# Loading the first 1 MB of a batch-norm kernel by four transfers of every fourth partition in place of one

## The chip, the cores and the metric

The kernel runs on one core of a Trainium2 chip. The metric is the device time in microseconds (us) of one launch. A profile of one execution shows a span (first to last instruction) that is some 1.8 us shorter than that time.

## The reference

```python
batch, channels, h, w = 32, 128, 32, 32      # x: 16.78 MB of float32
normalized = (x - running_mean) / np.sqrt(running_var + eps)
scaled = normalized * gamma + beta           # all per channel
return np.maximum(scaled, 0)
```

So 16.78 MB are read and 16.78 MB written, with a multiply-add and a maximum for each element in between.

## The kernel before

A row is one (batch, channel) image of 1,024 floats, 4 KB. Partition p holds 16 consecutive rows, 64 KB that are contiguous in HBM, and there are T = 2 such blocks. `PIECES` cuts the 16 rows of a block into pieces, the first ones small so that ScalarE can begin early. All loads are issued by SyncE, all stores and the four small parameter loads by ScalarE. Everything fits in SBUF at once, so no load waits for a buffer.

```python
PIECES = (((0, 2), (2, 4), (4, 8), (8, 16)), ((0, 8), (8, 16)))
STORE_CUTS = {(0, 1)}
...
for t in range(T):
    for a, b in PIECES[t]:
        xt = data.tile([P, b - a, HW], F32, name=f"x{t}_{a}")
        nc.sync.dma_start(out=xt, in_=xr[t, :, a:b, :])
        tiles.append((t, a, b, xt))
raw = params.tile([Q, 4, J], F32, name="raw")
for k, src in enumerate((running_var, gamma, running_mean, beta)):
    nc.scalar.dma_start(out=raw[:, k, :], in_=src.rearrange("(q j) -> q j", j=J))
...                                          # scale and bias of every channel
for t, a, b, xt in tiles:
    first = a
    for j in range(a, b):
        nc.scalar.activation(out=xt[:, j - a, :], in_=xt[:, j - a, :], func=ACTF.Relu,
                             bias=bias_t[:, j : j + 1], scale=scale_t[:, j : j + 1])
        if j + 1 == b or (t, j + 1) in STORE_CUTS:
            nc.scalar.dma_start(out=outr[t, :, first : j + 1, :], in_=xt[:, first - a : j + 1 - a, :])
            first = j + 1
```

The kernel names no semaphore. The framework hands out eight for the transfers of these two queues and reuses them; a transfer that gets a used one waits until the earlier transfer has landed.

## Time and profile before

| | before |
|---|---|
| time, median | 83.73 us (83.72 to 83.98, 3 runs) |
| span | 81.9 us |
| ScalarE busy | 38.5 us |
| share of the 16 DMA engines, loads + stores | 48.4% + 47.8% |
| first packet of x begins | 1.84 us |
| last completions of the 16 engines | 80.28 to 80.60 us |

The prediction shows the views. One more line is needed to compare with: how long SyncE's queue is busy with one issue. It comes from the view of the load's source line; the three durations are shortest, median and longest in ns, then the first and last start in us.

```profile
L52 SPq DMA_DIRECT2D x<-in_x_dram x6: 328/398/678, 0.8 to 8.0; - x6
```

The first three of these six, by the trace's records, began at 0.807, 1.229 and 1.706 us and took 372, 428 and 424 ns.

### The profile page before, as it was taken

What the parts mean: (1) busy time and instruction counts of PE and PEld (TensorE: products, weight loads), DVE (VectorE), ACT (ScalarE), POOL (GpSimd) and SP (SyncE); (2) the same over time, 40 slices, a digit from 0 to 9 for tenths busy, and PEclk for the clock granted to TensorE, in tenths of its full rate; (3) what the DMA queues carried; (4) which work ended last, traced back from release to release, by engine and by line L of the source; (5) the groups of instructions that cost most, each with busy time, mean ns of one, the idle gap of its engine ahead of it and who ended that gap; (6) DMA issues with size and microseconds to landing.
All of it is one profiled execution on the core that took longest, in us unless ns stands there. A gap on an engine that the chain in (4) does not pass through costs nothing.

```text
span 81.9 us, 119 instructions
## 1 busy us (share of the span) xinstructions
PE 0.7 (1%) x2; PEld 0.5 (1%) x2; DVE 0.8 (1%) x5; ACT 38.5 (47%) x34; POOL 0.8 (1%) x6
## 2 busy tenths in 40 slices
PE   0002000000000000000000000000000000000000
PEld 0002000000000000000000000000000000000000
DVE  0000300000000000000000000000000000000000
ACT  0600377799039999199994199993000000000000
POOL 3000000000000000000000000000000000000000
DMA  2899999989899999979789798996999899799690
GB/s 32 328 425 472 408 448 448 512 352 494 370 448 416 446 418 396 500 296 600 320 380 580 304 464 384 512 512 288 480 512 400 368 512 448 320 512 496 272 512 0
DMA packets 1936, 33.56 MB, mean 410 GB/s; under 512 B 272, under 2 KB 272, under 8 KB 528
## 3 DMA queue, kind: packets, MB, share of 16 engines
q1 hardware_dynamic: 864, 16.78, 48.4%
q10 hardware_dynamic: 1072, 16.78, 47.8%
HBM read 16.78 MB, written 16.78 MB: 410 GB/s over the span
## 4 chain that ended last, share of the span: by engine, by line
DMA 56%; ACT 11%; SPq 0%; issue 0%
DMA x<-in_x_dram 56%; ACT x L96 11%; SPq L52 0%
## 5 line engine op out<-in xcount | busy, mean ns | idle before, releaser
L96 ACT ACTIVATE x<-x,bias_t,scale_t 128x1024 f32<-128x1024 f32 x32 | 37.0, 1228 | 10.3 <-DMA x<-in_x_dram 7.9
L82 ACT ACT_TABLE_LOAD x1 | 1.3, 1283 | 2.6 <-issue 2.6
L82 ACT ACTIVATE std_t<-cols,eps_t 128x16 f32<-128x16 f32 x1 | 0.3, 273 | 4.5 <-PE cols L74 4.5
L74 PE MATMUL cols<-raw,rep 8*128 8x64 f32 x2 | 0.7, 428 | 7.7 <-DMA raw<-in_beta_dram 7.7
L74 PEld LDWEIGHTS cols<-raw,rep 8*128 8x128 f32 x2 | 0.5, 304 | 7.7 <-issue 7.7
L64 POOL TENSOR_SCALAR_AFFINE_SELECT rep<-rep 8x128 f32<-8x128 f32 x1 | 0.4, 392 | 0.1
L84 DVE RECIPROCAL rstd_t<-std_t 128x16 f32<-128x16 f32 x1 | 0.3, 254 | 7.8 <-ACT std_t L82 7.8
L63 POOL MEMSET rep<- 8x128 f32 x1 | 0.2, 195 | 0.3 <-POOLq L124 0.3
L86 DVE TENSOR_TENSOR scale_t<-cols,rstd_t 128x16 f32<-128x16 f32 x1 | 0.2, 175 | 0.1
L90 DVE TENSOR_TENSOR bias_t<-cols,ms_t 128x16 f32<-128x16 f32 x1 | 0.2, 175 | 0.0
L88 DVE TENSOR_TENSOR ms_t<-cols,scale_t 128x16 f32<-128x16 f32 x1 | 0.2, 175 | 0.0
L124 POOL MEMSET const-bfloat16-1.0<- 128x1 bf16 x1 | 0.1, 106 | 0.0
L124 POOL MEMSET const-uint8-127<- 128x1 uint8 x1 | 0.1, 106 | 0.0
L124 POOL MEMSET const-float32-0.0<- 128x1 f32 x1 | 0.1, 103 | 0.3 <-issue 0.3
L124 POOL MEMSET const-float32-1.0<- 128x1 f32 x1 | 0.1, 103 | 0.0
L61 DVE MEMSET eps_t<- 128x1 f32 x1 | 0.1, 59 | 0.9 <-PEq L124 0.9
## 6 DMA issues: line engine op xcount, KB each, us to landing
x<-in_x_dram SPq DMA_DIRECT2D x3, 4096.0 KB, 38.8
out_dram<-x ACTq DMA_DIRECT2D x3, 4096.0 KB, 27.9
x<-in_x_dram SPq DMA_DIRECT2D x2, 1024.0 KB, 5.7
x<-in_x_dram SPq DMA_DIRECT2D x1, 2048.0 KB, 11.2
out_dram<-x ACTq DMA_DIRECT2D x1, 2048.0 KB
out_dram<-x ACTq DMA_DIRECT2D x2, 512.0 KB, 18.8
out_dram<-x ACTq DMA_DIRECT2D x1, 1024.0 KB
raw<-in_running_var_dram ACTq DMA_DIRECT2D x1, 0.5 KB
```

The lines of the kernel that those rows point to most:

```text
L61: nc.vector.memset(eps_t, float(eps))
L63: nc.gpsimd.memset(rep, 1.0)
L64: nc.gpsimd.affine_select(out=rep, in_=rep, compare_op=mybir.AluOpType.is_equal, fill=0.0, base=0, pattern=[[0, P // Q], [-1, Q]], channel ...
L74: nc.tensor.matmul(cols.rearrange("p k j -> p (k j)"), rep.rearrange("q r s -> q (r s)"), raw.rearrange("q k j -> q (k j)"), start=True, s ...
L82: nc.scalar.activation(out=std_t, in_=cols[:, 0, :], func=ACTF.Sqrt, bias=eps_t[:, 0:1], scale=1.0)
L84: nc.vector.reciprocal(out=rstd_t, in_=std_t)
L86: nc.vector.tensor_mul(out=scale_t, in0=cols[:, 1, :], in1=rstd_t)
L88: nc.vector.tensor_mul(out=ms_t, in0=cols[:, 2, :], in1=scale_t)
L90: nc.vector.tensor_sub(out=bias_t, in0=cols[:, 3, :], in1=ms_t)
L96: nc.scalar.activation(out=xt[:, j - a, :], in_=xt[:, j - a, :], func=ACTF.Relu, bias=bias_t[:, j : j + 1], scale=scale_t[:, j : j + 1],)
L124: nc = _bacc.Bacc("TRN2", target_bir_lowering=False, num_devices=1)
```

## The change

The intent is to let all 16 DMA engines start sooner.

```diff
+SEED = 4
...
             xt = data.tile([P, b - a, HW], F32, name=f"x{t}_{a}")
-            nc.sync.dma_start(out=xt, in_=xr[t, :, a:b, :])
+            n = SEED if (t, a) == (0, 0) else 1
+            for s in range(n):
+                nc.sync.dma_start(out=xt[s::n], in_=xr[t, s::n, a:b, :])
```

## The prediction

> **What bounds the kernel now.** I read the view of cores first: 81.9 us from first to last instruction at clock 1.000, 1.83 us below the timed 83.73 us. I then read the page from the top, to see which engine could be the bound. No compute engine is: ScalarE is busy 38.5 us of 81.9, in 32 activations of 1.23 us, and everything else is under 1 us. The DMA rows of the page are different.
>
> ```profile
> DMA  2899999989899999979789798996999899799690
> ...
> DMA packets 1936, 33.56 MB, mean 410 GB/s; under 512 B 272, under 2 KB 272, under 8 KB 528
> ...
> q1 hardware_dynamic: 864, 16.78, 48.4%
> q10 hardware_dynamic: 1072, 16.78, 47.8%
> ```
>
> The first row is the mean share of the 16 DMA engines in 40 slices of 2.05 us: low in the first slice and zero in the last, and between them high, with dips that come from how a long packet is credited to slices. The two queues, loads (q1) and stores (q10), take 48.4 + 47.8 = 96.2% of the engines' span, 78.8 us. Only about 3.1 us of the whole program is not DMA time. Next I asked in which stretches it lies, by the busy time of the engines in chosen windows (columns: window, length, five engines' busy us and counts, clock, DMA share, GB/s; a packet's bytes are credited to the window in which it begins).
>
> ```profile
> 1.60:1.80 0.20, 0.00 (x0) 0.00 (x0) 0.00 (x0) 0.00 (x0) 0.00 (x0) 1.00 0.03 2
> 1.80:2.00 0.20, 0.00 (x0) 0.00 (x0) 0.00 (x0) 0.00 (x0) 0.00 (x0) 1.00 1.97 287
> 2.00:2.20 0.20, 0.00 (x0) 0.00 (x0) 0.00 (x0) 0.00 (x0) 0.00 (x0) 1.00 0.99 164
> 2.20:2.40 0.20, 0.00 (x0) 0.00 (x0) 0.00 (x0) 0.00 (x0) 0.00 (x0) 1.00 0.31 82
> 2.40:2.60 0.20, 0.00 (x0) 0.00 (x0) 0.00 (x0) 0.00 (x0) 0.00 (x0) 1.00 0.30 123
> 2.60:2.80 0.20, 0.00 (x0) 0.00 (x0) 0.00 (x0) 0.18 (x1) 0.00 (x0) 1.00 0.82 328
> 2.80:3.00 0.20, 0.00 (x0) 0.00 (x0) 0.00 (x0) 0.20 (x1) 0.00 (x0) 1.00 1.01 410
> 3.00:4.80 1.80, 0.00 (x0) 0.00 (x0) 0.00 (x0) 0.90 (x1) 0.00 (x0) 1.00 0.98 414
> 4.80:42.00 37.20, 0.65 (x2) 0.49 (x2) 0.78 (x4) 26.10 (x24) 0.00 (x0) 1.00 1.03 438
> 42.00:78.00 36.00, 0.00 (x0) 0.00 (x0) 0.00 (x0) 11.13 (x10) 0.00 (x0) 1.00 1.00 431
> ```
>
> From 3.0 us to 78 us the engines run at 414 to 438 GB/s without a hole; it matters little whether they carry loads, stores or both. Nothing moves before 1.8 us. Between 1.8 and 2.8 us is a ramp. Those two places, and some 1.3 us after the last packet, are all there is to win, and the change works on the ramp.
>
> The trace's packet records show the ramp in detail. Each of the first load's 128 partitions is one packet of 8 KB. The 16 engines begin their first one at 1.844 to 2.509 us: one after another, over 0.665 us. These first packets take 0.31 to 1.03 us where each later one takes 0.309 us; the early starters are the slow ones, and all 16 end between 2.670 and 2.998 us. After that each engine runs packet on packet: the 16 first-load completions leave at 4.836 to 5.136 us, and the very last completions of the program at 80.279 to 80.604 us. The spread among engines, 0.30 us at the beginning, is 0.33 us at the end. So each engine has its own chain of fixed work, and the program ends when the one that started worst ends. Its effective start is 5.136 - 8 x 0.309 = 2.66 us, and from there to 80.604 us it works 77.94 us. By packets of 32 KB at 1.21 us, its 2.10 MB would take 64 x 1.21 = 77.4 us, so it hardly ever idles.
>
> The page's chain of waits tells the same only in part:
>
> ```profile
> 0.81 0.37 SPq L52
> 1.18 0.05 issue
> 1.23 6.74 DMA x<-in_x_dram
> 7.97 0.02 issue
> 7.99 38.77 DMA x<-in_x_dram
> 46.76 0.03 issue
> 46.79 9.16 ACT x L96 x8
> ```
>
> It goes through the last load (issued at 7.99 us because its semaphore was in use) and the last eight activations, then stops at the last store, whose transfer it doesn't follow. I don't take this chain as the bound. When the last activation ends at 55.95 us, the store queue still holds about 6.4 MB: by then some (55.97 - 2.5) x 0.43 = 23.0 MB have moved, 16.78 MB of them loads, so 6.2 MB of the 12.6 MB of stores issued earlier. Earlier or later activations therefore wouldn't change the end.
>
> **What the skill says.** "DMA: Bandwidth & Descriptors", section "The descriptor swizzle", gives for a 128-partition transfer the engine of a partition as 8 * (partition >> 6) + ((partition >> 2) & 7): groups of four neighbours go to one engine. Every fourth partition then gives each of the 16 engines exactly two rows, which must be the reason for the stride. The same page, section "Why a DMA increments its semaphore by 16 and not by 1", has the number of engines as the largest k up to 16 that divides the slowest dimension of both sides; 32 rows still give 16. The trace of before agrees for 128 rows (16 engines, eight packets each); nothing in it shows 32. "SBUF — State Buffer", section "The DMA setup-cost knee", advises one large transfer in place of several because each pays about 2 us. That is latency of a single transfer; here the transfers overlap in the queue, and at the border of two loads (4.836 us) the next packet begins 6 ns after the completion packet, so I don't charge it. "Perfetto Trace Analysis", section "DMA Optimizations", says that splitting may let some transfers start sooner[...].
>
> **The change, part by part.** Removed: one 1 MB load. Added: four of 256 KB, so three more issues on SyncE's queue and 3 x 16 = 48 completion packets. Bytes, data packets (128 of 8 KB), activations and stores stay.
>
> *Gain.* The start-up stagger of 0.665 us belongs to 128 rows. If it goes with the rows, 32 rows take 0.665 / 4 = 0.17 us, and the last engine begins at 1.844 + 0.17 = 2.01 us in place of 2.509. In before the first packets end 0.16 to 0.49 us after the last engine has begun; the same here gives 2.17 to 2.50 us, so the worst engine gains 2.998 - 2.50 = 0.50 us. The most that is possible is a start of every engine at 1.844 us without slow packets: 2.66 - 1.84 = 0.82 us, 1.0% of the time. If the slow first packets come from something else (the generator still has the other 96 rows to do in the same 0.7 us, or the memory is slow at first whatever is asked), the gain is nearly 0. I take the middle, 0.28 us.
>
> *Cost on the engines.* Three more completions per engine, 9 ns each: 0.03 us, all on the path.
>
> *Issue.* SyncE's queue issued its first four loads at 0.81, 1.23, 1.71 and 2.21 us; issue to first packet was 1.844 - 0.807 = 1.04 us. So the four small loads bring packets from about 1.85, 2.27, 2.75 and 3.2 us, and the second piece, issued at about 2.65 us in place of 1.23, from 3.7 us. One small load is two packets per engine, 0.62 us, more than the 0.42 to 0.50 us between issues. An engine that ends its first packet at 2.5 us has work to 2.8, 3.4, 4.0 and 4.65 us: each next load is there 0.5 us or more before it is needed. No cost.
>
> *Compute.* The parameter loads, which end at 7.6 us and hold TensorE (7.7 us of wait), sat behind the first load's packets and may land earlier. Activations and stores then start earlier than 9.72 us. By the store backlog above this is worth nothing at the end.
>
> Sum: -0.28 + 0.03 = -0.25 us; 83.73 gives 83.48.
>
> **Rivals.** (1) *Nothing but reordering*: descriptor generation for 128 rows takes as long as before and the packets crawl until it is through; time 83.7 to 83.8. For it: the early starters' packets took up to 1.03 us while those that began at 2.41 us took 0.307 to 0.342. Against: engines that already have a full packet's descriptor should be able to run it. (2) *A wait for a semaphore starves the queue.* The kernel already shows such waits:
>
> ```profile
> SPq L52 <- DMA raw<-in_running_mean_dram: 4.1, 1, 4.1
> ...
> SPq L52 <- DMA x<-in_x_dram: 0.7, 1, 0.7
> ```
>
> Loads reuse semaphores of earlier transfers, and three more transfers bring reuse forward. If the second piece waits for the first small load (about 3.1 us), it's still in time at 4.1; if for the last one (about 5.0 us), the engines would stand still for some 1.4 us: 84.9. In before the first reuse waited for a parameter load that had landed at 2.19 us, so I expect the harmless kind. (3) *The 32 rows don't spread as I assume*, for instance so that two engines write to the same group of partitions at once or only eight engines work. 1 MB at half rate is 2.45 us more: 86.1. The stride looks chosen against this. (4) *The whole ramp is gained*: 82.9.
>
> **Range and chances.** Between rival 1 and the full stagger gain lie 83.2 to 83.8; a little more for (4) and for a mild form of (2) gives 82.95 to 83.95 as the range for 8 in 10. Faster by over 2% would need 1.67 us, twice the largest possible gain: 0.01. Slower by over 2% needs rival 3, or 2 at its worst: 0.04. The rest, 0.95, is within 2%.
>
> **What would show it.** Right: in the windows of the changed kernel, the rate from 2.0 to 2.8 us is up; the first completions of the last small load leave near 4.5 us in place of 4.836 to 5.136; the last packets end as much earlier; 1,984 DMA packets (48 more); queue shares as before; no hole between 3 and 5 us. Wrong: engines' first packets still ending near 2.7 to 3.0 us (rival 1), a hole near 4 to 6 us with a wait on SyncE's queue (rival 2), or packets of 8 KB at 0.6 us, or on fewer engines (rival 3).

## The result and the profile after

| | before | after |
|---|---|---|
| median of 6 runs | 83.77 us (83.72 to 84.06) | 87.45 us (86.88 to 87.70) |
| span | 81.9 us | 85.6 us |
| ratio | | 1.0426 (1.039 to 1.0462) |

A ratio here is the mean time of one kernel's runs over that of the other's runs of the same rounds, so not quite the ratio of the medians. Executions over 1.5% slower than the fastest of the same kernel are left out of the means. The predicted time was 83.48 us, with a range to 83.95: the change costs 3.7 us where a small gain was expected.

The page of the changed kernel, in the lines that answer to those of before:

```profile
DMA  0799999999999999999999899998999999999910
...
DMA packets 1984, 33.56 MB, mean 392 GB/s; under 512 B 320, under 2 KB 320, under 8 KB 576
...
q1 hardware_dynamic: 912, 16.78, 47.2%
q10 hardware_dynamic: 1072, 16.78, 45.7%
```

The 48 more packets are the completions of three more transfers. The row of shares now begins with an empty slice (2.14 us each). The row hardly shows the rest of the loss: it ends in 9, 1 and 0, although one engine works until 84.12 us, 1.5 us longer than the second last. The windows at the start say more (columns as in the prediction).

```profile
1.80:2.00 0.20, 0.00 (x0) 0.00 (x0) 0.00 (x0) 0.00 (x0) 0.00 (x0) 1.00 0.01 0
2.00:2.20 0.20, 0.00 (x0) 0.00 (x0) 0.00 (x0) 0.00 (x0) 0.00 (x0) 1.00 0.95 205
...
2.60:2.80 0.20, 0.00 (x0) 0.00 (x0) 0.00 (x0) 0.09 (x1) 0.00 (x0) 1.00 0.68 287
2.80:3.00 0.20, 0.00 (x0) 0.00 (x0) 0.00 (x0) 0.20 (x1) 0.00 (x0) 1.00 0.40 165
3.00:4.80 1.80, 0.00 (x0) 0.00 (x0) 0.00 (x0) 0.99 (x1) 0.00 (x0) 1.00 0.84 265
4.80:6.60 1.80, 0.65 (x2) 0.49 (x2) 0.00 (x0) 0.27 (x1) 0.00 (x0) 1.00 0.93 341
6.60:8.40 1.80, 0.00 (x0) 0.00 (x0) 0.78 (x4) 0.00 (x0) 0.00 (x0) 1.00 0.99 405
8.40:42.00 33.60, 0.00 (x0) 0.00 (x0) 0.00 (x0) 21.25 (x19) 0.00 (x0) 1.00 1.02 432
```

No packet of a load begins before 2.0 us, where before had 287 GB/s from 1.8 us on. From 3.0 to 4.8 us the rate is 265 GB/s against 414 in before, and it doesn't reach 430 until after 8 us. The share of busy engines (0.84, then 0.93) falls less than the rate: engines stand still, and besides that packets take longer. After the first packets the fifth microsecond is the worst. Here it is in before, then in the changed kernel:

```profile
4.00:5.00 1.00, 0.00 (x0) 0.00 (x0) 0.00 (x0) 0.00 (x0) 0.00 (x0) 1.00 1.01 418
```

```profile
4.00:5.00 1.00, 0.00 (x0) 0.00 (x0) 0.00 (x0) 0.00 (x0) 0.00 (x0) 1.00 0.83 205
```

By the packet records, all 64 packets of the first two small loads had begun by 3.80 us, and no further packet of data began before 4.02 us. The view of the load's line shows the issues:

```profile
L57 SPq DMA_DIRECT2D x<-in_x_dram x9: 328/542/602, 0.8 to 25.4; - x9
```

By the trace's records the four small loads were issued at 0.806, 1.407, 2.030 and 2.658 us and took 542, 573, 586 and 602 ns; the second piece followed at 3.304 us. The chain of waits, cut to its long steps, ends with ScalarE as before:

```profile
2.66 5.95 DMA x<-in_x_dram
...
25.43 27.59 DMA x<-in_x_dram
...
54.19 8.01 ACT x L101 x7
```

Its last load was issued at 25.43 us, in place of 7.99, since it waited for the semaphore of the first store. That looks grave and isn't: the engines moved 424 GB/s from 20 to 30 us, since earlier loads and the stores kept them busy.

**Where 3.7 us went.** I added up the packet records. "Nominal" is what an engine's packets take at their usual durations (8 KB 0.306 us, 32 KB 1.21 us from start to start). "Slow" is what packets took beyond that, "idle" is the rest, both as the mean of the 16 engines; "last" is how much later than the mean the last engine was done.

```
                        begin  nominal  slow  idle  mean end  last   last end
before                   1.84   77.73   0.64  0.22   80.42    0.18    80.60
after                    2.12   77.74   1.38  0.80   82.04    2.08    84.12
difference              +0.28   +0.01  +0.74 +0.58   +1.62   +1.90    +3.52
```

With 0.16 us more between the last packet and the end of the program (1.45 against 1.29 us), these are the 3.7 us of the two spans. A late begin, slow packets and idle engines cost 1.62 us on average, and a single engine loses 1.90 us more. A packet is counted as slow by its length in the trace; whether it was moving or waiting in that time, the record doesn't tell. The slow part is 0.70 us higher between 4 and 12 us alone. That one engine fell behind early: 15 of the 16 completions of the fourth small load landed between 5.73 and 6.95 us, the last at 8.60. By chaining its packets (the records don't name the engine, so this is a reconstruction), this engine began that load's first packet at 6.36 us, and this packet took 1.46 us. It stayed behind to the end.

### The profile page after: what moved, and what is told of

The parts are those of the page before. It is cut to its first block, busy times and chain, and to the rows that moved or that the text cites. A ratio compares the mean times of both kernels' runs of the same rounds, so it can differ in the third digit from the quotient of the medians.

```text
span 85.6 us, 122 instructions
## 1 busy us (share of the span) xinstructions
PE 0.7 (1%) x2; PEld 0.5 (1%) x2; DVE 0.8 (1%) x5; ACT 38.5 (45%) x34; POOL 0.8 (1%) x6
## 4 chain that ended last, share of the span: by engine, by line
DMA 57%; ACT 11%; SPq 2%; issue 2%; ACTq 0%
DMA x<-in_x_dram 39%; DMA out_dram<-x 18%; ACT x L101 11%; SPq L57 2%; ACTq L101 0%
```

## The experiments

I formed the theories at the traces. **A**: a transfer costs SyncE's queue and what generates its descriptors about the same whatever its rows, and 256 KB (0.62 us of work for the engines) is too little for that cost. **B**: the step of four partitions makes the issue slow. **C**: the parameter loads on ScalarE's queue, issued in the same 3 us, get in the way. A and B both mean starvation: engines that run dry. The rival to both is that stepped transfers move badly in themselves.

### Four transfers without a step over partitions

```diff
-nc.sync.dma_start(out=xt[s::n], in_=xr[t, s::n, a:b, :])
+nc.sync.dma_start(out=xt[:, j, k : k + c], in_=xr[t, :, a + j, k : k + c])   # 128 partitions, 2 KB each; cut: the if around it
```

> The first piece in four transfers of all 128 partitions and 2 KB each (halves of its two rows), so no step over partitions. Theory A (each transfer costs SyncE's queue and the descriptor generator about 0.55 to 0.6 us whatever its rows, so four of 256 KB starve the engines): issues stay at 0.54 to 0.60 us, second piece issued at about 3.3 us, time 86.5 to 88. Theory B (the step of four partitions makes the issue slow): issues fall to the 0.37 to 0.43 us of before, second piece issued at about 2.6 us, time 83.5 to 84.3 (2 KB packets may cost up to 0.4 us).

85.68 us, ratio 1.0205 (1.0179 to 1.0232). The four issues took 371 to 472 ns, so B is right on what makes an issue slow. But the time didn't go back: half of the loss remains, with 0.54 us idle and 1.41 us slow per engine and a last engine 1.35 us behind. Both theories had a miss. Most of what the average engine lost here is slow packets (+0.77 us on before), not idle time (+0.32 us); the profiled execution is the slowest of the four, 86.20 us. It is not the plain cost of smaller packets: those of 2 KB mostly took 84 ns and followed each other at about 78 ns, four of them 0.31 us, as one of 8 KB.

### Four blocks of neighbouring partitions

```diff
-xt[s::n], in_=xr[t, s::n, a:b, :]
+xt[s * m : s * m + m], in_=xr[t, s * m : s * m + m, a:b, :]                  # m = 32
```

> Four transfers of 32 neighbouring partitions each. Theory A: issues of 0.54 to 0.60 us as in the changed kernel, time 86.5 to 88. Theory B: issues of 0.4 us; the time then depends on how 32 neighbours are spread: near 83.7 if over 16 engines, 85 to 87 if over eight at a time.

85.75 us, ratio 1.0225 (1.0207 to 1.0243). The issues were fast again (371 to 468 ns). The first two windows here are from 3 to 5 us:

```profile
3.00:4.00 1.00, 0.00 (x0) 0.00 (x0) 0.00 (x0) 0.79 (x1) 0.00 (x0) 1.00 0.98 205
4.00:5.00 1.00, 0.00 (x0) 0.00 (x0) 0.00 (x0) 0.00 (x0) 0.00 (x0) 1.00 1.12 247
```

The engines are all busy at half the rate: packets of 8 KB took about 0.6 us until 7 us. This agrees with the Trainium skill, "SBUF — State Buffer", section "Door 1: The DMA port swizzle (why `[64,N]` ≈ `[32,N]`)": partitions 0 to 31 reach 8 of 16 ports, measured there at 189 GB/s. This is rival 3 of the prediction, but in this kernel and not in the changed one, where 86 of the first 128 packets took at most 0.315 us. Nothing there points to a bad spread of the rows.

### Two stepped transfers in place of four

```diff
-SEED = 4
+SEED = 2
```

> Two transfers of every second partition (64 rows) in place of four. Theory A: one extra issue of 0.55 to 0.6 us, but each brings 512 KB, 1.2 us of work, so the engines don't run dry: 83.5 to 84.3. Theory B: a step of two slows the issue too; with two slow issues in place of four, about half of the loss: 85 to 86.

85.66 us, ratio 1.0222 (1.0185 to 1.0259). That is B's number, about half of the loss: issues of 538 and 575 ns, and the next two (of whole pieces, without a step) at 578 and 505 ns still slow behind them. First packet at 2.12 us, mean end 0.92 us later than before, last engine 1.00 us behind the mean.

### The parameter loads on another queue

```diff
-nc.scalar.dma_start(out=raw[:, k, :], ...)
+nc.gpsimd.dma_start(out=raw[:, k, :], ...)
```

> The changed kernel with the four parameter loads issued on GpSimd's queue, so that SyncE's queue is alone at the start. Theory C (the generator is shared with ScalarE's queue, and the eight issues of the first 3 us hold each other up): SyncE's issues fall to 0.33 to 0.40 us, second piece issued at about 2.3 us, time 83.3 to 84.3. Theories A and B: issues stay at 0.54 to 0.60 us, time 86.5 to 88.

> Control: the kernel before with only the parameter loads moved to GpSimd's queue. Both theories: the time of before, 83.5 to 84.2; it's the base of the run above and of the run with the changed kernel's parameters moved.

Applied to the changed kernel: 86.69 us, ratio 1.0344 (1.0302 to 1.0387), issues still 547 to 593 ns. Applied to the kernel before: 84.34 us, ratio 1.006 (1.0043 to 1.0078). This control came out a little above its expected range. C is refuted for the issues. Against its control the change now costs 2.35 us in place of 3.7, so the parameter loads may have had a share. The mean end lies 1.80 us after that of its control (82.67 and 80.87), much as the 1.62 us of the change itself; only the last engine is less far behind (1.59 us in place of 2.08). The profile is of the slowest of four executions (87.26 us), so these ends say a little too much.

### The cost of one transfer by itself

Five kernels put six tiny transfers of 512 B per row ahead of the loads, with the parameter loads on GpSimd's queue. Only the partitions and HBM rows differ.

```diff
+for i in range(6):
+    s = i % 4
+    probe = data.tile([P, 128], F32, name=f"probe{i}")
+    nc.sync.dma_start(out=probe[s::4], in_=xr[0, s::4, i, :128])   # or 32*s : 32*s+32, or all
```

> A measurement by itself: the kernel before with the parameter loads on GpSimd's queue and, ahead of its loads, six tiny transfers of 512 B from every fourth partition (32 rows, 16 KB) on SyncE's queue. The data take almost no engine time, so the distance of the landings is what one such transfer costs the generator. Theory B (a stepped transfer costs about 1 us of generation, which starved the engines in the changed kernel): landings 0.8 to 1.1 us apart, issues 0.54 to 0.60 us. Theory A (0.55 to 0.6 us for any transfer): landings as far apart as in the two probes without a step.

> The same six tiny transfers from 32 neighbouring partitions. Theory B: landings 0.40 to 0.45 us apart, issues 0.37 to 0.43 us. Theory A: the same distance as with the step.

> The same six tiny transfers from all 128 partitions (64 KB each). If generation goes with the rows, four times the distance of the 32 neighbouring rows or more; if it is per transfer, the same 0.40 to 0.45 us. The prediction had assumed 0.67 us for 128 rows and a quarter for 32.

> Six tiny transfers of 512 B rows written to every fourth partition, but read from 32 neighbouring rows. If the step on the SBUF side is what makes the issue slow: issues 0.54 to 0.60 us and landings 0.63 us apart; if the step on the HBM side: 0.37 to 0.43 us and 0.47 us.

> The mirror: read from every fourth row of HBM, written to 32 neighbouring partitions. If the step on the SBUF side is the cause: issues 0.37 to 0.43 us and landings 0.47 us apart; if that on the HBM side: 0.54 to 0.60 us and 0.63 us.

The view of the probes' line, first with the step on both sides:

```profile
L51 SPq DMA_DIRECT2D probe<-in_x_dram x6: 542/590/595, 0.8 to 3.9; - x6
```

32 neighbouring partitions:

```profile
L51 SPq DMA_DIRECT2D probe<-in_x_dram x6: 377/417/423, 0.8 to 3.1; - x6
```

All 128 partitions:

```profile
L51 SPq DMA_DIRECT2D probe<-in_x_dram x6: 371/429/432, 0.8 to 3.1; - x6
```

Step on the SBUF side alone:

```profile
L51 SPq DMA_DIRECT2D probe<-in_x_dram x6: 542/590/594, 0.8 to 3.9; - x6
```

Step on the HBM side alone:

```profile
L51 SPq DMA_DIRECT2D probe<-in_x_dram x6: 378/417/425, 0.8 to 3.1; - x6
```

The distance between the complete landings, over the last five of the six, is (6.10 - 2.91) / 5 = 0.64 us with the step, (4.90 - 2.54) / 5 = 0.47 us with 32 neighbours and (5.33 - 2.79) / 5 = 0.51 us with 128 rows. So: four times the rows cost next to nothing more; the step costs 0.17 us per transfer; and nearly all of that cost is on the SBUF side (0.64 us for the step on that side alone, from 2.86 to 6.06; 0.50 us for the step on the HBM side, from 2.38 to 4.88). The stepped probes also begin 0.32 us later (first packet 2.14 against 1.82 us). The 0.8 to 1.1 us that B had in mind is too much, and the "same for all" of A is wrong too: the step costs something, and so does any transfer, each less than claimed. The landings are about as far apart as the issues (0.63 and 0.46 us from issue to issue, with the step and with 32 neighbours), so the probes don't tell a slow issue from a slow generation of descriptors. The times (88.88, 87.46, 87.33, 88.47 and 87.76 us, in the order of the expectations above) only say that six more transfers ahead of everything cost some microseconds.

### The same split with a full queue in front

First at the end, on the last load of 4 MB:

```diff
-n = SEED if (t, a) == (0, 0) else 1
+n = SEED if (t, a) == (1, 8) else 1
```

> The same split in four by every fourth partition, but of the last load (4 MB in four times 1 MB), which waits behind a full queue. If the loss of the changed kernel is starvation at the start (A and B alike), it is hidden here: 83.6 to 84.3. If stepped transfers themselves move their packets slowly or load the engines unevenly, 85 or more, with packets of 32 KB above 1.21 us or one engine ending over 1 us after the others.

84.58 us, ratio 1.0094 (1.0067 to 1.0122), a little over what starvation alone allowed. The engines ended within 0.41 us of each other. The quarters were issued at 8.1, 25.1, 25.6 and 45.1 us, held by reused semaphores (35.3 us of waiting for stores on SyncE's queue), and load packets after 20 us were slower by 0.28 us per engine (0.42 against 0.14). That is no mark of the step: by the same count the two kernels without any split that serve as controls have 0.55 and 0.52 us.

Then on the second piece, right behind an unsplit first one:

```diff
+n = SEED if (t, a) == (0, 2) else 1
```

> The same four stepped transfers of 256 KB, but of the second piece: the first 1 MB goes in one transfer as before, so every engine has 2.5 us of work queued when the slow issues begin. Starvation theory (the loss comes from engines that run dry because 256 KB is only 0.62 us of work against about 0.64 us of generation): the loss vanishes or falls to that of the late split, 83.7 to 84.6, no idle stretch before 8 us, last packets of all engines within 0.5 us. If stepped transfers near the start are bad in themselves (slow packets, one late engine), 85 to 87 as in the changed kernel.

85.63 us as the median of three executions (a fourth, 87.31 us, was slow), ratio 1.0245 (1.0194 to 1.0297). Taken at its word this supports the rival. But the waits on SyncE's queue show something else in the way:

```profile
SPq L57 <- DMA x<-in_x_dram: 3.9, 3, 2.5
```

The fourth small load got the semaphore of the first piece and waited 2.5 us for its landing, to 5.50 us; from 6.5 us to 7.5 us the rate fell to 287 GB/s. So the run may have been confounded by rival 2 of the prediction. It isn't settled that this wait explains the loss: by the sums of above, idle time is hardly more than in before (0.3 us at most, against 0.22), and what grew is slow packets (1.8 us per engine, against 0.64). With the parameter loads moved to GpSimd's queue, their semaphores are free for the loads, and none waits until the first 4 MB load:

> The split of the second piece again, with the parameter loads on GpSimd's queue, so that no load up to the 2 MB one waits for a reused semaphore (in the run before, the fourth small load waited until 5.5 us and the engines ran dry at 6.8). Every engine has 2.5 us of work queued before the first small transfer. Starvation theory: no engine runs dry, 83.7 to 84.4. If the stepped transfers are slow in themselves near the start (slow packets although the queue is full): 85 to 86.5.

84.16 us, ratio 1.0034 (1.0018 to 1.0051), against 84.34 us for its control without any split. The four stepped issues were as slow as ever (526 to 677 ns), and it no longer mattered. These two kernels and the changed one with its parameter loads moved are alike but for the split: none 84.34 us, second piece 84.16, first piece 86.69. From 3 us on:

```profile
3.00:4.00 1.00, 0.00 (x0) 0.00 (x0) 0.00 (x0) 0.00 (x0) 0.92 (x4) 1.00 0.92 385
4.00:5.00 1.00, 0.00 (x0) 0.00 (x0) 0.00 (x0) 0.00 (x0) 0.18 (x1) 1.00 1.04 434
```

Idle is 0.16 us per engine (0.13 in the control) and the last engine is 0.38 us behind the mean. Some packets of the stepped loads were slow although the queue was full: 0.26 us per engine between 4 and 8 us, 0.01 in the control. So much of the rival's slow packets is left with a full queue. Over the whole program slow packets are no more than in the control (1.05 and 1.18 us).

### The same four stepped transfers, twice as large

```diff
-PIECES = (((0, 2), (2, 4), (4, 8), (8, 16)), ...
+PIECES = (((0, 4), (4, 8), (8, 16)), ...        # in the changed kernel, and in the kernel before
```

> The first two pieces merged into one of 2 MB, and this split in four by every fourth partition: the same number of stepped transfers at the same place, but 512 KB each, 1.22 us of work against 0.64 us of generation. Starvation theory: the first issue is still slow (+0.3 us) but nothing runs dry later: 83.9 to 84.7. If the number of stepped transfers at the start is what costs, whatever their size: 86 to 88.

> Control for the run above: first two pieces merged, not split. One transfer fewer than before; the engines are busy all the same: 83.5 to 84.0 in either theory.

Split: 85.41 us, ratio 1.0188 (1.0163 to 1.0214). Its control, not split: 84.10 us, ratio 1.0037 (1.0018 to 1.0055), just above its expected range. So with 512 KB per transfer the split costs 1.3 us instead of 3.7. That is far from "whatever their size", but more than I allowed: the first packet is late as always (2.13 us), idle fell to 0.25 us, yet slow packets (0.43 us per engine from 4 to 8 us) and a last engine 0.88 us behind the mean remain.

### Two transfers without a step

> The first piece in two transfers without a step (its two rows of 4 KB, 128 partitions each). Starvation theory with the step as its cause: 512 KB is 1.22 us of work against 0.47 us of generation, so nothing runs dry: 83.6 to 84.2. If any split of the first piece costs, as the four column transfers (85.68) make one suspect: 84.6 to 85.7, with slow packets between 3 and 8 us.

84.43 us, ratio 1.0072 (1.0055 to 1.0089), the column split above with `SEED = 2`, two transfers of 512 KB. A little over the range of starvation by the step, and short of "any split costs".

## Why the prediction was wrong

**What bounds the kernel** was right, and it is what made the change expensive: each engine has a fixed amount of work, and what the start lost was paid at the end. The last packets ended 3.5 us later, and nothing in between gave any of it back. Also right: activations that start earlier (8.71 us in place of 9.72; the parameter loads were through by 5.6 instead of 7.7 us) were worth nothing, and three more completions per engine cost next to nothing (9 ns each in the trace, 0.03 us as predicted).

**The step that failed first** is the gain: "If it goes with the rows, 32 rows take 0.665 / 4 = 0.17 us". It doesn't. The engines began the first small load between 2.12 and 2.80 us: over 0.68 us, the stagger of 128 rows. The probes say the same of whole transfers, 0.47 us for 32 rows and 0.51 for 128. And the load began 0.28 us later, which no rival had. (The 0.28 us of gain was also called the middle between 0 and 0.50 us, which is 0.25; nothing hangs on it.) One sign of being right came true and misled: from 2.0 to 2.8 us the rate was up, 215 against 174 GB/s, but before had moved packets since 1.84 us and was still ahead.

**The step that failed at greater cost** is the issue: "each next load is there 0.5 us or more before it is needed. No cost." I had taken the 0.42 to 0.50 us between issues, and the 1.04 us from an issue to its first packet, from transfers without a step. The stepped issues came 0.60 to 0.65 us apart. That alone is about the 0.62 us of work in 256 KB, a shortfall of 0.03 us at most for each. The delay from issue to first packet grew as well: the third small load was issued at 2.03 us, in place of 1.71, and its first packet (the 65th of the loads) began at 4.02 us, 1.99 us later. Engines that had finished the second small load stood idle. Nine of the next 32 packets took 0.6 us or more, and the second piece was issued at 3.30 us and not at 2.65. So the path that failed is the supply of packets from the queue to the engines, which the prediction had as always ahead. Why the third load came so late stays open.

How size and step go with the loss can be read from the splits of the same 1 MB:

```
ratio to before     no step            step over partitions
2 x 512 KB          1.0072 (columns)   1.0222
4 x 256 KB          1.0205 (columns)   1.0426
```

Either halving the parts or adding the step takes the loss from 0.7% to about 2%, and both together to 4.3%. The cells differ in more than that (packets of 4, 2 and 8 KB, a step of two or of four), so this is a guide and no clean division.

What is shown is where the loss belongs: to a split with nothing queued in front of it. With the parameter loads on GpSimd's queue in all three, the split of the first piece costs 2.35 us and that of the second piece, behind 1 MB of work, nothing that can be measured (86.69 and 84.16 against 84.34 us). What is not shown is that the distance between issues starves the engines. The columns were issued 0.42 to 0.52 us apart, faster than their 0.62 us of work, and lost 2.05% all the same; four stepped transfers with 1.22 us of work each still lost 1.3 us. In the changed kernel slow packets (+0.74 us) and idle engines (+0.58 us) both count.

**The rivals.** Rival 1 (nothing but reordering) had the first half of the mechanism, packets that crawl at the start. Rival 2 (a reused semaphore) did not strike in the changed kernel: the second piece's issue was not held, and the later waits fell after 3 MB of further loads had been issued. A wait of its kind did occur in the first split of the second piece. Rival 3 (bad spread) was right not to be expected with the step: each small load posted 16 completions and most packets ran at full speed. The neighbouring blocks show what it would have been. The chance of 0.04 for a loss over 2% was wrong because both rivals that led there were judged on their own, and a late supply in the new form was not among them.

**What stays open.** First, why one engine falls 2 us behind: its late packet is seen, and that it goes along with the loss (0.38 us behind the mean with a full queue, 0.88 with 512 KB, 2.08 with 256 KB), but not why that engine. Second, the supply in the changed kernel was slower than the probes allow: the third tiny stepped transfer had landed at 4.01 us, while the third small load of 8 KB rows landed from 4.98 to 6.32 us. And the column transfers of 256 KB lost time although tiny transfers of 128 rows land only 0.51 us apart. So the supply also depends on something that the 512 B probes don't have; the bytes of a row are an obvious guess, and no run here tests it. The parameter loads are another: with them on GpSimd's queue the stretch from 3.8 to 4.4 us had 260 GB/s in place of 138, but the idle total stayed about the same. Third, the slow packets of stepped loads, at the start and behind a full queue.

No version beat the kernel before. The two controls (84.10 and 84.34 us), the late split, the second one of the second piece and the two columns lie within 1% above it, which counts as the same where 2% is asked for.

## What to carry to other kernels

Before you split a transfer at the start of a program, compare the work in each part (bytes over the engines' rate) with the distance between issues, and with the delay from an issue to its first packet, measured for exactly that form. Enough work per part is not a guarantee: here parts with 1.22 us of work, issued 0.59 to 0.64 us apart, still lost 1.3 us. The same split behind one unsplit transfer of 1 MB cost nothing that could be measured. In the probes a step over partitions made an issue of 0.43 us into one of 0.59 us, and the number of rows hardly mattered, so fewer rows per transfer was not a cheaper transfer. Where the bytes bound a kernel, what the slowest engine loses at the start is still missing at the end: here it landed its share of the fourth small load 1.65 us after all others, and ended 1.5 us after all others.

## What the Trainium skill lacked or had wrong

- No page has that a step over partitions on the SBUF side slows a load's issue on SyncE's queue: 542 to 595 ns against 371 to 432 ns, and landings 0.64 us apart against 0.47 to 0.51. A step on the HBM side alone costs nothing of this kind (378 to 425 ns). It belongs to "DMA: Bandwidth & Descriptors".
- "DMA: Bandwidth & Descriptors", section "Latency and other measured facts", gives about 600 ns to the first byte on this path. From the start of the issue to the first packet the trace has 1.04 us (before) and 1.32 us (with the step). The page doesn't say from where it counts; from the end of the issue it is 0.67 and 0.77 us, near the page. What it lacks is that the third stepped load in a row took 1.99 us from the start of its issue.
- "Perfetto Trace Analysis", section "DMA Optimizations", says that splitting may let some transfers start sooner, and that it may help where the DMA engines are generally idle. They were not: loads and stores took 96.2% of their time. The page has nothing on a kernel whose engines are idle at its start alone; here four parts of 256 KB cost 4.3%, and four columns without a step 2.05%.
- "SBUF — State Buffer", section "The DMA setup-cost knee", advises one large transfer, and that was the better choice here. Its 2 us for a transfer are seen in the tiny probes (1.6 to 2.2 us from issue to landing). How far several of them overlap is not on the page: here they landed 0.47 to 0.64 us apart.
- For a load of 32 stepped partitions no page says how the rows go to the engines. The formula that the prediction used is given for 128 partitions. Here each such load posted 16 completions, and 86 of the first 128 packets took at most 0.315 us for 8 KB.
